# Splitting the out-projection's weights on GpSimd instead of ACT, DVE and SP

## The chip, the cores and the metric

The kernel runs on one core of one Trainium2 chip. Its time is the device time of one execution in microseconds, lower is better; each kernel is run several times and the median is given. The engines are TensorE (PE: matmuls), VectorE (DVE), ScalarE (ACT), GpSimd (POOL) and SyncE (SP). Each engine works its own queue in order. SP's queue does nothing here but issue DMA transfers; POOL's queue holds arithmetic and DMA issues together.

## What is computed

One decoder layer on a sequence of 1024 tokens and a model width of 1024, in float32. The core of the reference, cut down:

```python
h = rms_norm(x, pre_g)
z = einsum('bsd,de->bse', h, w_in)                 # in-projection, width 7184
qa, ka, va, ga, qb, kb, vb, gb, gk_low = split_columns(z)
oa = diff_attention(qa, ka, va, lam)               # 8 heads, two softmax maps each
oa = rms_norm(oa, subln_g) * (1 - lam_init) * silu(ga)
ob = gla_chunked(qb, kb, vb, log_a)                # 4 heads, gated linear attention
ob = rms_norm(ob, gla_g) * silu(gb)
y = einsum('bse,ed->bsd', concatenate([oa, ob]), w_out)   # out-projection, 2048 x 1024
return x + rms_norm(y, post_g)
```

## The kernel before

TensorE multiplies numbers of a shortened float32 form (`fp32r`). To keep the precision, each operand is split into two such parts: the high part is the value cast to `fp32r` (`act.copy(hi, raw)`), the low part is the value minus the high part (`dve.tensor_tensor(lo, raw, hi, subtract)`). A product is then three matmuls: high by high, low by high, high by low.

The in-projection runs from the start to about 630 us. It goes through the columns of `w_in` in pairs of blocks, with a scheme of seven block products for each pair in place of eight (the steps n = 1, 2, 5, 6, 4, 7, 3 of the list `order`). For each step, `make_weights` takes a raw block of `w_in` (tile `w_raw`), for some steps forms a difference of blocks on DVE (line 296), and splits it (line 315 on ACT, line 316 on DVE) into a tile `w`. There are five such tiles (`NRING = 5`), and `go` prepares the weights of up to three steps ahead before it issues a step's matmuls (`multiply`, line 117). A step is 12 matmuls with 512 columns (24 with 256 columns for the values).

Results leave PSUM in `step`: ACT copies one product to an SBUF tile `s` (line 427), and DVE adds another product from PSUM to it (line 440) into a tile `c`. Then `take` finishes the block (for instance scale, gate or split) and SP stores it to DRAM. The tile `c` comes from a group of four buffers with the tag "c":

```python
def t_c(name, dt=F32):
    return t2k("c", 4, name, dt)
```

Beside the in-projection runs the gated linear attention (`gla`, fed by `fill`): among its steps is a causal mask on POOL (`pool.affine_select`, line 775, tile `gan`), which TensorE's products `gpo` read later.

In the same stage the weights of the out-projection, `w_out`, are split ahead of time, so that the later stage can load finished high and low parts. This is `wo_step`. The matrix is cut into 32 pieces of 128 rows and 512 columns (256 KB each). The steps n = 2 and n = 4 of a pair load one piece into the tile `wo_raw`, of which there is one buffer (tag "t4", `bufs=1`); the steps n = 1 and n = 6 split the piece that is loaded: the high part goes to a tile `wo_hi`, taken from the four buffers of tag "c", the low part is written over the raw piece. Both are stored to DRAM (`wod`). So the next load waits until the low part's store is done.

Which buffer a tile gets, and the order of the instructions on each queue, is not written by hand. A planner goes through the program at build time with its own estimates of each instruction's cost, and lets the instruction go first that is ready and comes earlier in the program. Only TensorE's matmuls and a few instructions (`tc.keep_in_program_order`) hold the order of the program. At run time every queue keeps the order that was planned, and each instruction waits by semaphores for what it needs.

The finished parts are read back by `weights` (line 910): the pieces of the rows 1024 to 2047 on POOL's queue from about 602 us, the others on SP's from about 806 us. From 630 us on come the attention (scores, softmax, values) and the out-projection in turns.

Of the kernel before, what the change touches and what calls it, by code (L numbers as in the profile page):

```python
# [11 lines left out]
ALU = mybir.AluOpType  # L12
PSUM = bass.MemoryType.PSUM

P = 128
# [16 lines left out]
def hymba_kernel(  # L32
# [21 lines left out]
    act, dve, pool, pe, sp = nc.scalar, nc.vector, nc.gpsimd, nc.tensor, nc.sync  # L54

    def fp(t):
        return t.bitcast(F32)

    def cols(half):
        return slice(half * 512, half * 512 + 512)  # L60
# [38 lines left out]
    wod = [tc.dram_tile([2, P, D], F32, name=f"wo{e}_d") for e in range(2 * D // P)]  # L99
# [60 lines left out]
    def t_c(name, dt=F32):  # L160
        return t2k("c", 4, name, dt)
# [418 lines left out]
    def wo_step(n):  # L580
        if n in (1, 6) and wo_open:
            e, dh, raw = wo_open.pop()
            hi = t_c("wo_hi", F32R)
            act.copy(hi, raw)
            lo = raw.bitcast(F32R)
            dve.tensor_tensor(lo, raw, fp(hi), ALU.subtract)
            for t, src in enumerate((hi, lo)):
                sp.dma_start(wod[e][t][:, cols(dh)], fp(src))
        if n in (2, 4) and wo_todo:
            e, dh = wo_todo.pop(0)  # L590
            raw = ap.tile([P, 512], F32, tag="t4", name="wo_raw", bufs=1)
            sp.dma_start(raw, w_out[0, e * P : (e + 1) * P, cols(dh)])
            wo_open.append((e, dh, raw))

    def go(n):
        for _ in range(n):
            i = made[0]
            if i == len(order):
                return
            made[0] = i + 1  # L600
            for a in range(4):
                prepare(i + a)
            step(i)
            if order[i][0] > EARLY and not (wide(order[i][0]) and order[i][0] % 2):
                wo_step(order[i][1])
            if fill and next(fill[0], 0) == 0:
                fill.pop(0)
# [918 lines left out]
```

## Time and profile before

| | us |
|---|---|
| median of 3 runs | 980.15 |
| lowest and highest of them | 979.73 and 980.77 |
| the profiled execution's own time | 979.08 |
| its span in the profile | 977.4 |

Engine busy times in the profile are sums over instructions. A line such as "L584 ACT CAST wo_hi<-wo_raw 128x512" names the line of the kernel, the engine, the operation, the tile that is written and the tile that is read, and the shape (partitions x elements). Where a wait is shown with "<-", the name behind the arrow is what ended it. A DMA's busy time on its queue is only the issue; the time to landing is given apart. The granted clock of TensorE is given as a share of the full one.

### The profile page before, as it was taken

To read this page: it belongs to the slowest core of one execution; us is meant where nothing else is said; L and a number is where in the kernel's file an instruction comes from. 1 tells how busy PE (TensorE), PEld (TensorE's weight loads), DVE (VectorE), ACT (ScalarE), POOL (GpSimd) and SP (SyncE) were. 2 spreads that over 40 slices of the span, in tenths; PEclk is the share of its full clock that TensorE was granted. 3 is DMA by queue.
4 is the path that set the end of the run, shared out by engine and by line. 5 is a ranking of instruction groups with operands and counts; after the bars stand their busy time and mean duration, and the time that the engine had idled before them with its cause. 6 is when DMAs were issued, how large, how long until landed. Compare 5 with 4: busy or idle time off the path is not lost.

```text
span 977.4 us, 15766 instructions
## 1 busy us (share of the span) xinstructions
PE 956.7 (98%) x5338; PEld 830.4 (85%) x5338; DVE 735.4 (75%) x1452; ACT 600.5 (61%) x1164; POOL 142.9 (15%) x158
## 2 busy tenths in 40 slices
PE   5999999999999999999999999999999999999997
PEld 5998988888889998999888888878888888888785
DVE  6887597789866667686786876487888888898554
ACT  8742455487357455454665775366776687887773
POOL 4300000000000010000200002121322222443321
PEclk9999999999999999999999999999999999999999
DMA  9432446656774868897987866987656669994677
GB/s 345 151 110 91 139 135 205 231 179 225 238 247 162 264 187 286 254 294 229 293 259 243 273 202 191 407 269 272 197 186 228 240 199 344 340 294 105 151 208 147
DMA packets 152593, 220.45 MB, mean 226 GB/s; under 512 B 17104, under 2 KB 83664, under 8 KB 152416
## 3 DMA queue, kind: packets, MB, share of 16 engines
q1 hardware_dynamic: 146176, 203.71, 64.1%
q0 software_dynamic: 6336, 15.73, 7.0%
q8 instruction: 42, 0.69, 0.3%
q14 instruction: 39, 0.32, 0.1%
HBM read 133.93 MB, written 88.60 MB: 228 GB/s over the span
## 4 chain that ended last, share of the span: by engine, by line
PE 95%; DVE 2%; ACT 1%; DMA 1%; issue 1%; POOL 0%; SPq 0%; DVEq 0%; ACTq 0%; POOLq 0%
PE x L117 24%; PE y L117 15%; PE z L117 15%; PE ypart L117 13%; PE sc L117 7%; PE po L117 5%; PE yps L117 4%; PE wtr L120 3%; PE gpo L117 3%; PE kv L117 1%; PE gkl_ps L117 1%; PE pa L117 1%; DMA x<-in_x_dram 1%; PE xT L120 1%; DVE s_lo L548 0%
## 5 line engine op out<-in xcount | busy, mean ns | idle before, releaser
L315 ACT CAST w<-w_raw 128x512 fp32r<-128x512 f32 (+1 forms) x164 | 112.4, 688 | 94.7 <-PE y L117 44.1
L316 DVE TENSOR_TENSOR w<-w_raw,w 128x512 fp32r<-128x512 f32 (+1 forms) x164 | 126.7, 774 | 50.1 <-ACT w L315 43.3
L1049 ACT ACTIVATE p<-p,stt 128x896 f32<-128x896 f32 (+7 forms) x128 | 99.3, 777 | 36.7 <-DVE stt L1039 33.9
L427 ACT COPY s<-x 128x512 f32<-128x512 f32 x84 | 49.1, 585 | 84.4 <-PE x L117 84.3
L775 POOL TENSOR_SCALAR_AFFINE_SELECT gan<-gan 128x512 f32<-128x512 f32 x8 | 16.5, 2060 | 485.4 <-ACT gan L774 449.8
L296 DVE TENSOR_TENSOR w_raw<-w_raw 128x512 f32<-128x512 f32 (+1 forms) x96 | 75.9, 791 | 13.9 <-DMA w_raw<-in_w_in_dram 12.6
L1039 DVE CUSTOM_DVE_ANT_0 p<-sc,maskt 128x512 f32<-128x512 f32 (+3 forms) x128 | 74.3, 585 | 14.5 <-PE sc L117 13.3
L117 PE MATMUL ypart<-wo_hi,m_hi 128*128 128x512 f32 x192 | 79.5, 414 | 0.1
L117 PE MATMUL y<-h_hi,w 128*128 128x512 f32 x320 | 79.6, 391 | 0.0
L117 PE MATMUL z<-s_hi,w 128*128 128x512 f32 x320 | 79.6, 391 | 0.0
L117 PE MATMUL x<-s_hi,w 128*128 128x512 f32 x320 | 79.6, 391 | 0.0
L1055 POOL TENSOR_SCALAR p<-p,stt,lam 128x1024 f32<-128x1024 f32 (+3 forms) x64 | 56.2, 879 | 146.9 <-DVE stt L1054 141.9
L117 PE MATMUL ypart<-wo_hi,m_lo 128*128 128x512 f32 x192 | 75.5, 393 | 0.0
L117 PE MATMUL ypart<-wo_lo,m_hi 128*128 128x512 f32 x192 | 75.4, 393 | 0.0
L117 PE MATMUL sc<-k,q 128*128 128x512 f32 (+1 forms) x192 | 69.0, 363 | 1.3 <-DVE stt L1039 1.2
L117 PEld LDWEIGHTS x<-s_hi,w 128*128 128x128 f32 x320 | 59.7, 188 | 12.2
L117 PEld LDWEIGHTS y<-h_hi,w 128*128 128x128 f32 x320 | 59.6, 188 | 12.2
L117 PEld LDWEIGHTS z<-s_hi,w 128*128 128x128 f32 x320 | 59.5, 188 | 12.0
L117 PE MATMUL sc<-ks,q 128*128 128x512 f32 (+1 forms) x192 | 66.1, 347 | 0.0
L1097 ACT CAST wt_hi<-wtr 128x512 fp32r<-128x512 f32 (+1 forms) x80 | 42.7, 534 | 24.6 <-PE wtr L120 23.8
L1098 DVE TENSOR_TENSOR wt_lo<-wtr,wt_hi 128x512 fp32r<-128x512 f32 (+1 forms) x80 | 50.7, 633 | 8.6 <-ACT wt_hi L1097 8.0
L1058 DVE SCALAR_TENSOR_TENSOR p<-p,stt,p 128x1024 f32<-128x1024 f32 (+3 forms) x64 | 52.1, 814 | 4.1 <-POOL p L1055 3.9
(226 smaller groups left out, 2247.7 us busy)
## 6 DMA issues: line engine op xcount, KB each, us to landing
w_raw<-in_w_in_dram SPq DMA_DIRECT2D x56, 512.0 KB, 4.7
wo_raw<-in_w_out_dram SPq DMA_DIRECT2D x32, 256.0 KB, 3.0
wo_d<-wo_hi SPq DMA_DIRECT2D x32, 256.0 KB, 2.8
wo_d<-wo_raw SPq DMA_DIRECT2D x32, 256.0 KB, 3.8
q<-q_d SPq DMA_DIRECT2D x32, 256.0 KB, 4.7
k<-k_d SPq DMA_DIRECT2D x32, 256.0 KB, 5.7
ks<-k_d SPq DMA_DIRECT2D x64, 128.0 KB, 6.2
v<-v_d SPq DMA_DIRECT2D x16, 512.0 KB, 7.0
```

Of the source, the lines that this page charges most:

```text
L117: tc.keep_in_program_order(pe.matmul(*a, **k))
L120: tc.keep_in_program_order(pe.transpose(dst, src, ident))
L296: dve.tensor_tensor(dst, a, b, ALU.subtract)
L315: act.copy(w[0], src)
L316: dve.tensor_tensor(w[1], src, fp(w[0]), ALU.subtract)
L427: act.copy(b[k], ps)
L1039: ins = dve.tensor_tensor_reduce(p[:, a:e], sc[:, : e - a], maskt[:, NZ + P - (e - a) :] if last else maskt[:, : e - a], 1.0, 3e38 if i == ...
L1049: act.activation(p[:, :n], p[:, :n], AF.Exp, bias=st[:, m : m + 1], scale=-1.0, accum_out=st[:, 2 + m : 3 + m],)
L1055: pool.tensor_scalar(p1[:, :n], p1[:, :n], st[:, 5:6], lam, ALU.mult, ALU.mult)
L1058: dve.scalar_tensor_tensor(p0[:, :n], p0[:, :n], st[:, 4:5], p1[:, :n], ALU.mult, ALU.subtract)
L1097: act.copy(hi[:, :n], pt[:, :n])
L1098: dve.tensor_tensor(lo[:, :n], pt[:, :n], fp(hi[:, :n]), ALU.subtract)
```

## The change

The 32 pieces of `w_out` are handled by POOL alone. The load of a piece, the cast to the high part, the difference that is the low part and the two stores all go to POOL's queue: 32 loads, 32 casts, 32 differences and 64 stores. ACT, DVE and SP have none of it. The buffers, their tags and their counts, and the places of the calls in the program stay as they are.

```diff
@@ wo_step @@
         if n in (1, 6) and wo_open:
             e, dh, raw = wo_open.pop()
             hi = t_c("wo_hi", F32R)
-            act.copy(hi, raw)
+            pool.tensor_copy(hi, raw)
             lo = raw.bitcast(F32R)
-            dve.tensor_tensor(lo, raw, fp(hi), ALU.subtract)
+            pool.tensor_tensor(lo, raw, fp(hi), ALU.subtract)
             for t, src in enumerate((hi, lo)):
-                sp.dma_start(wod[e][t][:, cols(dh)], fp(src))
+                pool.dma_start(wod[e][t][:, cols(dh)], fp(src))
         if n in (2, 4) and wo_todo:
             e, dh = wo_todo.pop(0)
             raw = ap.tile([P, 512], F32, tag="t4", name="wo_raw", bufs=1)
-            sp.dma_start(raw, w_out[0, e * P : (e + 1) * P, cols(dh)])
+            pool.dma_start(raw, w_out[0, e * P : (e + 1) * P, cols(dh)])
             wo_open.append((e, dh, raw))
```

## The prediction

> **What bounds the kernel now.** I read the page's head first, then the waits of TensorE, then the busy time by stretches. The head gives the span and the engines' shares.
>
> ```profile
> span 977.4 us, 15766 instructions
> PE 956.7 (98%) x5338; PEld 830.4 (85%) x5338; DVE 735.4 (75%) x1452; ACT 600.5 (61%) x1164; POOL 142.9 (15%) x158
> ```
>
> The view of waits, for TensorE alone (engine and line, what it waited for, us in total, times, longest):
>
> ```profile
> PE xT L120 <- DVE x L482: 9.4, 4, 7.2
> PE y L117 <- DVE s L565: 1.3, 1, 1.3
> PE sc L117 <- DVE stt L1039: 1.2, 2, 0.9
> PE y L117 <- ACT s L427: 0.7, 1, 0.7
> PE x L117 <- ACT h_hi L521: 0.6, 1, 0.6
> PE po L117 <- ACT wt_hi L1097: 0.5, 1, 0.5
> ```
>
> The stretches. The splits of the out-projection's weights run from 158 to 556 us.
>
> ```profile
> core 0: us, PE busy (x) PEld busy (x) DVE busy (x) ACT busy (x) POOL busy (x), PEclk, DMA share, GB/s
> 0.00:30.00 30.00, 20.02 (x125) 18.22 (x126) 19.81 (x40) 24.37 (x47) 16.90 (x23) 1.00 0.99 345
> 158.00:300.00 142.00, 142.00 (x656) 118.60 (x655) 110.90 (x178) 83.42 (x145) 0.66 (x1) 1.00 0.66 223
> 300.00:560.00 260.00, 260.00 (x1662) 236.24 (x1661) 188.29 (x286) 146.36 (x256) 15.82 (x7) 1.00 0.79 251
> 632.00:977.00 345.00, 336.84 (x1743) 283.62 (x1741) 267.70 (x719) 245.84 (x553) 98.09 (x106) 1.00 0.76 229
> ```
>
> TensorE is the bound. While the splits run it is busy 142.00 of 142 us and 260.00 of 260 us, at the full clock (1.00). DVE and ACT work beside it with room left (110.90 and 83.42 of 142). POOL is nearly idle there: 0.66 us of work in 142. The reader should take one thing from this: there is no idle time of TensorE between 158 and 560 us for the change to take away, only idle time that it can add.
>
> **What is taken off ACT and DVE.** The tile view of the raw weight gives the two arithmetic steps (ns min/median/max).
>
> ```profile
> L584 ACT CAST wo_hi<-wo_raw x32: 603/621/622, 158.4 to 553.8; 128x512 fp32r<-128x512 f32 x32
> L586 DVE TENSOR_TENSOR wo_raw<-wo_raw,wo_hi x32: 680/687/695, 159.2 to 554.4; 128x512 fp32r<-128x512 f32 x32
> ```
>
> ACT loses 32 x 0.621 = 19.9 us and DVE 32 x 0.687 = 22.0 us. Both lie wholly beside a TensorE that never waits here, so I count them at 0. If that cover were missing, 22 us is the most they could be worth.
>
> **What is taken off SP.** 96 transfers leave SP's queue: 32 loads and 64 stores. From the waits of SP:
>
> ```profile
> SPq L588 <- ACT wo_hi L584: 53.5, 22, 5.8
> SPq L592 <- DMA wo_d<-wo_raw: 52.3, 27, 4.2
> ```
>
> SP stood 105.8 us behind these two steps. Queued behind them were the next in-projection weights and the stores of finished blocks. All of that still came in time, since TensorE shows no wait, so this too counts 0.
>
> **What POOL gets.** On POOL one piece is a serial chain, because the raw buffer is single and everything is on one in-order queue: load lands, cast, difference, two stores issued, the store of the low part lands, next load. I price each link by the nearest rows. Transfers first (KB each, median us from issue to landing):
>
> ```profile
> wo_raw<-in_w_out_dram SPq DMA_DIRECT2D x32, 256.0 KB, 3.0
> wo_d<-wo_hi SPq DMA_DIRECT2D x32, 256.0 KB, 2.8
> wo_d<-wo_raw SPq DMA_DIRECT2D x32, 256.0 KB, 3.8
> ...
> y_d<-yst SPq DMA_DIRECT2D x16, 256.0 KB, 4.4
> ...
> y_d<-yst POOLq DMA_DIRECT2D x16, 256.0 KB, 5.1
> ```
>
> The last two rows are the same 256 KB from the two queues: POOL's lands 5.1 - 4.4 = 0.7 us later (it also accumulates, so 0.7 may be too much). I add 0.7: load 3.7, high part 3.5, low part 4.5. The bounds are 0 and the whole 5.1 for each. The Trainium skill, in "DMA: Bandwidth & Descriptors", section "Latency and other measured facts", gives a first byte at about 1 us from GpSimd's queue and 0.6 us from SP's, so about 0.4 us later; by that the chain below would be 11.5 us and the loss about 2.6 us instead of 11.1.
>
> POOL's arithmetic, by shape (count, busy us, mean ns):
>
> ```profile
> L1147 POOL TENSOR_TENSOR gate<-r,gate 128x512 f32<-128x512 f32 x14 | 18.5, 1323 | 41.0 <-DVE r L1146 31.2 <-DVE stt L1054 9.8
> L775 POOL TENSOR_SCALAR_AFFINE_SELECT gan<-gan 128x512 f32<-128x512 f32 x8 | 16.5, 2060 | 485.4 <-ACT gan L774 449.8 <-DMA wo_d<-wo_hi 35.5
> ...
> L910 POOL DMA_DIRECT2D wo_lo<-wo_d x8 | 4.3, 534 | 3.0 <-PE x L117 1.4 <-PE y L117 0.8 <-DMA wo_lo<-wo_d 0.7
> ```
>
> No POOL cast of 128x512 stands in the trace. The nearest row is L775: one input of the same size, in the same stage. Its spread matters:
>
> ```profile
> L775 POOL TENSOR_SCALAR_AFFINE_SELECT gan<-gan x8: 659/1397/5553, 280.2 to 543.7; 128x512 f32<-128x512 f32 x8
> ```
>
> Alone it takes 0.66 us, in the median 1.40, at worst 5.55. The worst one shows why:
>
> ```profile
> 470.46 5.55 POOL L775 TENSOR_SCALAR_AFFINE_SELECT gan<-gan 128x512 f32<-128x512 f32 x1 [37.79 <-ACT gan L774]
> ```
>
> ```profile
> 474.23 1.29 DVE L316 TENSOR_TENSOR w<-w_raw,w 128x512 fp32r<-128x512 f32 x2
> 475.55 1.73 DVE L296 TENSOR_TENSOR w_raw<-w_raw 128x512 f32<-128x512 f32 x2
> ```
>
> DVE ran differences of two SBUF operands back to back up to 475.5; POOL ended 0.5 us after the first gap, and the next DVE pair took 1.73 us instead of 1.29. So POOL waits for a gap in such DVE work, and then DVE waits for POOL. The Trainium skill says the same in "SBUF — State Buffer", section "Who interferes with whom": a VectorE instruction with two SBUF inputs and a GpSimd instruction that reads SBUF shut each other out for a whole instruction; the trace agrees with its 5.55 us. What it would do to DVE is a rival below.
>
> I take 1.4 us for the cast (0.66 to 2.06) and 1.3 + 0.7 = 2.0 us for the difference (1.3 alone; 0.7 is the same wait, 1.40 - 0.66; at most 1.3 + 1.4). An issue from POOL is 0.53 us. The chain: 3.7 + 1.4 + 2.0 + 0.53 + 4.5 = 12.13 us a piece. The bounds: 3.0 + 0.66 + 1.3 + 0.53 + 3.8 = 9.3 and 5.1 + 2.06 + 2.7 + 0.53 + 5.1 = 15.5.
>
> **Against what pace.** The casts of before, from the timeline (start, us): piece 1, piece 15 and the last, piece 32.
>
> ```profile
> 158.43 0.62 ACT L584 CAST wo_hi<-wo_raw 128x512 fp32r<-128x512 f32 x1
> ```
>
> ```profile
> 300.13 0.60 ACT L584 CAST wo_hi<-wo_raw 128x512 fp32r<-128x512 f32 x1
> ```
>
> ```profile
> 553.79 0.62 ACT L584 CAST wo_hi<-wo_raw 128x512 fp32r<-128x512 f32 x1 [1.67 <-DMA wo_raw<-in_w_out_dram]
> ```
>
> The first 14 intervals take 141.7 us, 10.1 each; the later 17 take 253.7, 14.9 each. A chain of 12.13 falls behind by 2.01 us a piece (12.13 - 10.12) in the first stretch, 28.1 us by its end, and catches up in the second. Pieces late in themselves cost nothing: what they make is read after 600 us. The way to TensorE is the high part's buffer. It is one of four of tag "c", shared with the sums of finished blocks. Its reuse, from the timeline (in between come three other takings of such a buffer):
>
> ```profile
> 196.71 0.62 ACT L584 CAST wo_hi<-wo_raw 128x512 fp32r<-128x512 f32 x1
> ```
>
> ```profile
> 212.81 0.69 DVE L440 TENSOR_TENSOR c<-y,s 128x512 f32<-128x512 f32 x1 [1.57 <-ACT s L427]
> ```
>
> The buffer is wanted again 16.1 us after its cast began; on POOL it is held 1.4 + 2.0 + 3.5 = 6.9 us. So 9.2 us of lag are free. Beyond it the sum L440 waits on DVE, and behind it stand the weights' low parts (L316). Weights are made up to 3 steps ahead; a step is half of this row of the chain of waits:
>
> ```profile
> 185.06 5.44 PE x L117 x24
> ```
>
> That is 3 x 2.72 = 8.2 us more cover. What is left reaches TensorE: 28.1 - 9.2 - 8.2 = 10.7 us.
>
> Also queued behind POOL's waits are the eight masks L775. The worst of before began at 470.46, and its reader is
>
> ```profile
> 482.42 0.38 PE L117 MATMUL gpo<-gan,gv 128*128 128x128 f32 x2
> ```
>
> so a mask may come 12.0 - 0.66 = 11.3 us late; a piece's load or store wait (3.7 or 4.5 us) is inside that.
>
> The first load of all goes out late, since SP has much to issue before it:
>
> ```profile
> 19.82 0.60 SPq L592 DMA_DIRECT2D wo_raw<-in_w_out_dram  x1
> ```
>
> On POOL it has nothing before it and may go out while the first rows of x arrive. 256 KB at 345 GB/s is 0.76 us; TensorE's first wait (9.4 us, for x) could grow by 0 to 0.76. I take 0.4.
>
> **The sum.** 10.7 + 0.4 = 11.1 us. The profiled execution took 979.08 us (span 977.4 and 1.68 around it); the median of the runs is 980.15, so 1.07 us above it. On the median: 980.15 + 11.1 = 991.3 us. With the short chain of 9.3 nothing falls behind and nothing is lost; with 15.5 it is 5.4 x 14 - 17 = 58 us.
>
> **The rivals.**
> First, no change: the order of every queue is worked out by a planner at build time. If it prices POOL's chain about as long as it is, it gives later buffers to the pieces and no one waits; 32 x 12.1 = 387 us fit into the 395 from 158.43 to 553.79. A chain under 10.1 + 17.4 / 14 = 11.3 us gives the same. For it speaks the low bound of 9.3 and that lateness is free; against it that ACT stood before the last cast for the load to land (1.67 us in the row of 553.79), so the order of before already expects transfers quicker than they are. Time: 980.15 + 0.4, about 980.5.
> Second, DVE becomes late by the shared access, not by the buffer. While POOL works on a piece (1.3 + 0.66 us, waits not counted) DVE's two-operand work stands; 0.69 us of DVE goes away. That is 1.3 us more of DVE a piece at worst, 18 in the first 14: 129 of 142 us. It still fits on average; if two thirds of it fall where DVE has no room, 12 - 8.2 = 4 us are lost: 984.
> Third, the masks: if POOL lags by more than 11.3 us, each of eight makes TensorE wait, say 2.5 us: 20 us, 1000.
> Fourth, faster: SP, freed of 105.8 us, and ACT and DVE bring everything earlier. The waits that TensorE still has behind the first piece are sc 1.2 and po 0.5: 1.7 us, and 345 - 336.84 = 8.2 us of idle in the last stretch, of which a third might move by another order: at best 3 us, 977. It decides if POOL's chain stays under 10.1 and the start doesn't pay.
>
> **How the numbers follow.** The forecast, a chain too long that holds the buffers, 0.50; no change 0.33; DVE 0.08; masks 0.04; faster 0.05. A difference of 0.2% (2 us) is about what a measurement of this kernel can tell from no change. Slower by more: 0.50 + 0.08 + 0.04 = 0.62; within: 0.33; faster: 0.05. The forecast's own range is 983 to 1015 (chains of 11.5 to 13.8); with no change in it the range is 979 to 1015, which leaves out the faster case and the longer chains, some 0.1 more.
>
> **What would show it.** Right: a chain of 11.5 us or more from load to load on POOL in 158 to 300; new waits of DVE L440 for the transfer wo_d<-wo_hi; TensorE waits for DVE or ACT of about 10 us in all between 158 and 320; later steps of before shifted by as much. Wrong: TensorE still at 142 of 142 us; or the loss in another stretch (after 632, or at the start by more than 0.8); or TensorE waiting for L775.

## The result: 983.3 us, slower by 0.29%, and the profile after

| | before | after |
|---|---|---|
| median of 6 runs each, us | 979.94 | 983.28 |
| lowest and highest, us | 979.08, 980.77 | 982.41, 984.87 |
| ratio of the times, 95% interval | | 1.0029 [1.0018, 1.0039] |
| profiled execution: own time, span, us | 979.08, 977.4 | 983.59, 981.8 |

The change costs 3.3 us. The forecast had the sign, and 11.1 us. The page's head after, the span and the engines' totals:

```profile
span 981.8 us, 15766 instructions
PE 959.2 (98%) x5338; PEld 830.7 (85%) x5338; DVE 745.8 (76%) x1420; ACT 585.5 (60%) x1132; POOL 268.2 (27%) x318
```

Look at DVE. It was 735.4 us and gave away 32 differences, 22.0 us, so 713.4 were to be expected. It shows 745.8. Its remaining work became 32.4 us longer, 1.01 us for each piece. That is more than the 0.69 it was relieved of.

The view of waits for TensorE after (us in total, times, longest):

```profile
PE xT L120 <- DVE x L482: 8.9, 4, 7.2
PE x L117 <- ACT s L427: 1.6, 1, 1.6
...
PE z L117 <- DVE c L440: 0.3, 1, 0.3
PE z L117 <- DVE c L411: 0.3, 1, 0.3
```

The second, third and fourth of these lines are new: 2.2 us in three waits. They are short. The stretches:

```profile
0.00:30.00 30.00, 20.19 (x118) 18.17 (x119) 19.28 (x39) 24.36 (x47) 18.42 (x24) 1.00 1.00 356
...
158.00:300.00 142.00, 140.10 (x637) 115.81 (x636) 114.14 (x162) 70.10 (x121) 54.05 (x65) 1.00 0.63 207
300.00:560.00 260.00, 259.69 (x1650) 235.09 (x1649) 191.77 (x268) 140.56 (x241) 81.83 (x97) 1.00 0.79 253
```

TensorE, 142.00 of 142 before, has 140.10 now; in the next stretch 259.69 of 260. DVE went up from 110.90 to 114.14 in the first stretch although it has 14 differences less to do.

TensorE executes the same instructions in the same order in every kernel of this study, so two traces can be laid beside each other one matmul at a time. The table gives by how much a kernel's matmuls start later than in the trace of before, at some points of before's time (us). It is worked out from the starts in the traces; each is one execution.

| kernel | 30 | 150 | 220 | 246 | 335 | 420 | 560 | 595 | 660 |
|---|---|---|---|---|---|---|---|---|---|
| after | +0.9 | +0.8 | +0.8 | +3.6 | +4.1 | +4.1 | +4.6 | +4.6 | +4.4 |
| noread11 | +0.7 | +0.7 | +0.7 | +0.7 | +0.7 | +0.9 | +0.9 | +0.9 | +0.6 |
| own_hi | -0.4 | +3.2 | +3.2 | +3.7 | +3.7 | +5.1 | +5.1 | +5.1 | +4.7 |
| own_twice | +0.4 | +5.9 | +6.1 | +8.2 | +8.2 | +9.2 | +9.5 | +9.5 | +10.0 |
| late89 | 0.0 | 0.0 | 0.0 | 0.0 | 0.0 | 0.0 | 0.0 | +7.1 | +7.8 |
| late89_own | -0.4 | +3.0 | +3.0 | +3.9 | +3.9 | +5.5 | +5.5 | +5.5 | +5.1 |
| own_noread | +0.3 | +1.5 | +1.5 | +1.5 | +9.3 | +9.3 | +9.3 | +9.3 | +8.9 |
| dma_again | -0.5 | +0.7 | +0.7 | +0.7 | +0.8 | +2.6 | +2.6 | +2.6 | +2.3 |
| cast_sp | -0.8 | -0.8 | -0.8 | -0.8 | -0.8 | -0.8 | -0.8 | -0.8 | -0.8 |
| diff_sp | -0.9 | -0.9 | -0.9 | +0.3 | +0.3 | +2.2 | +2.2 | +2.2 | +2.5 |

After: 0.9 us are there by 30 us, and 2.8 come between 220 and 246. In that second place POOL, DVE, ACT and TensorE read as follows. POOL's timeline, one whole piece from load to load (start, us):

```profile
236.06 0.54 POOL L592 DMA_DIRECT2D wo_raw<-in_w_out_dram  x1 [5.33 <-DMA wo_d<-wo_raw]
239.13 0.70 POOL L584 CAST wo_hi<-wo_raw 128x512 fp32r<-128x512 f32 x1 [2.52 <-DMA wo_raw<-in_w_out_dram]
239.91 1.60 POOL L586 TENSOR_TENSOR wo_raw<-wo_raw,wo_hi 128x512 fp32r<-128x512 f32 x1
241.47 0.56 POOL L588 DMA_DIRECT2D wo_d<-wo_hi  x1
242.02 0.54 POOL L588 DMA_DIRECT2D wo_d<-wo_raw  x1
245.84 0.54 POOL L592 DMA_DIRECT2D wo_raw<-in_w_out_dram  x1 [3.27 <-DMA wo_d<-wo_raw]
```

DVE in the same microseconds:

```profile
238.67 0.68 DVE L375 TENSOR_TENSOR c<-c,g 128x512 f32<-128x512 f32 x1
239.27 1.10 DVE L382 SCALAR_TENSOR_TENSOR c<-c,b 128x512 f32<-128x512 f32 x1
240.29 1.77 DVE L375 TENSOR_TENSOR c<-c,g 128x512 f32<-128x512 f32 x1
...
243.80 0.68 DVE L440 TENSOR_TENSOR c<-z,s 128x512 f32<-128x512 f32 x1
```

The same operation of line 375 takes 0.68 us at 238.67 and 1.77 us at 240.29, while POOL's difference runs (239.91 to 241.51). With line 382 (1.10; 0.69 at most in before), which began beside POOL's cast, DVE loses 1.09 + 0.41 = 1.5 us in this one piece. It has no gap from 238 to 245.6 in which to make it up. Then ACT, and TensorE behind it:

```profile
244.51 0.63 ACT L372 ACTIVATE g<-c 128x512 f32<-128x512 f32 x1 [4.47 <-DVE c L440]
...
245.71 0.57 ACT L427 COPY s<-x 128x512 f32<-128x512 f32 x1
```

```profile
246.33 2.12 PE L117 MATMUL x<-s_hi,w 128*128 128x512 f32 x8 [1.57 <-ACT s L427]
```

ACT's gate (line 372) waits for DVE's late sum, the copy that TensorE needs stands two places behind it in ACT's queue, and TensorE stops for 1.57 us: about the 1.5 us that DVE was held up. This is one reading of one trace. The experiments ask whether it is the cause.

### The profile page after: what moved, and what is told of

Its sections match the earlier page's. It is cut to its first block, busy times and chain, and to the rows that moved or that the text cites. A ratio compares the mean times of both kernels' runs of the same rounds, so it can differ in the third digit from the quotient of the medians.

```text
span 981.8 us, 15766 instructions
## 1 busy us (share of the span) xinstructions
PE 959.2 (98%) x5338; PEld 830.7 (85%) x5338; DVE 745.8 (76%) x1420; ACT 585.5 (60%) x1132; POOL 268.2 (27%) x318
## 4 chain that ended last, share of the span: by engine, by line
PE 86%; DVE 7%; ACT 3%; issue 2%; DMA 2%; SPq 0%; POOL 0%; DVEq 0%; ACTq 0%; POOLq 0%
PE x L117 21%; PE ypart L117 13%; PE y L117 13%; PE z L117 13%; PE sc L117 7%; PE po L117 5%; PE yps L117 4%; PE wtr L120 3%; PE gpo L117 3%; DVE w L316 1%; PE kv L117 1%; PE gkl_ps L117 1%; DVE w_raw L296 1%; PE pa L117 1%; DMA x<-in_x_dram 1%
## 5 line engine op out<-in xcount | busy, mean ns | idle before, releaser
L316 DVE TENSOR_TENSOR w<-w_raw,w 128x512 fp32r<-128x512 f32 (+1 forms) x164 | 138.7, 848 | 59.5 <-ACT w L315 48.5
L584 POOL CAST wo_hi<-wo_raw 128x512 fp32r<-128x512 f32 x32 | 32.4, 1012 | 240.3 <-DMA q_d<-c 113.1
L296 DVE TENSOR_TENSOR w_raw<-w_raw 128x512 f32<-128x512 f32 (+1 forms) x96 | 80.0, 833 | 20.9 <-DMA w_raw<-in_w_in_dram 19.3
```

The source lines that it names most:

```text
L296: dve.tensor_tensor(dst, a, b, ALU.subtract)
L316: dve.tensor_tensor(w[1], src, fp(w[0]), ALU.subtract)
L584: pool.tensor_copy(hi, raw)
```

## The experiments

Four theories are named in the expectations. Theory 1: POOL's reads of SBUF hold up DVE. Theory 2: the forecast's, POOL's chain of loads and stores holds a shared buffer too long. Theory 3: the planner's other order on ACT and DVE. Theory 4 (for one kernel): loads from POOL's queue land late and hold up ACT's queue. Each group of kernels ran on one chip beside the kernel before; the ratios are to it.

### Only the reads, in the order of before

To the kernel before is added POOL work that nobody uses, behind each low store; all other queues have the order of before. `dummy_read` has two operations: the first reads the constant tile `maskt` and one column of a piece's high half, the second both tiles whole. `dummy_write` has one-column work and four writes of zeros.

```diff
+ pool.tensor_scalar(maskt[:, :512], maskt[:, :512], fp(hi)[:, 0:1], None, ALU.mult)       # dummy_read
+ pool.tensor_tensor(maskt[:, :512], maskt[:, :512], fp(hi), ALU.mult)
+ for _ in range(4): pool.memset(maskt[:, :512], 0.0)                                       # dummy_write
```

> The kernel before, plus 32 pairs of POOL instructions that read the high part and a constant tile of zeros and write the zeros back: one of one tile input, one of two, 128x512 each, as the change's cast and difference. ACT, DVE, SP and PE keep the order of before; the pieces stay on ACT, DVE and SP. Theory 1 (POOL's reads shut DVE out): each pair costs DVE about 1.0 us, as the change did (745.84 - 735.39 + 22.0 = 32.4 us in 32 pieces); DVE, which keeps its own 22 us, is busy about 768 us and the time is 983 to 988. Theory 2 (the pieces' chain on POOL is late and holds a buffer of tag c): no such chain here, 980 within 1. Theory 3 (the planner's other order on ACT and DVE): the order is that of before, 980 within 1.

> As dummy_read, but POOL only writes: after each piece a one-column product and four memsets of 128x512, about as long on POOL. Theory 1: writes alone shut nobody out; DVE busy within 3 us of before's 735.4, time 980 within 1. Theories 2 and 3: 980 within 1 too. If POOL's mere work cost time, it would be as slow as dummy_read.

Measured: dummy_read 981.85 us, ratio 1.0023 [1.0011, 1.0034]; dummy_write 980.28 us, 1.0005 [0.9994, 1.0016]. The two heads' lines, reads first:

```profile
PE 957.5 (98%) x5338; PEld 829.9 (85%) x5338; DVE 762.0 (78%) x1452; ACT 599.9 (61%) x1164; POOL 272.7 (28%) x222
```

```profile
PE 958.0 (98%) x5338; PEld 831.0 (85%) x5338; DVE 735.7 (75%) x1452; ACT 600.1 (61%) x1164; POOL 230.9 (24%) x318
```

Reads make DVE 26.6 us longer (0.83 us a pair of operations), writes do nothing to it. Theory 1's effect exists, without another order or another queue for the DMAs. Its price in the total is 2.0 us there, less than theory 1 expected, and 1.6 us more than dummy_write, with intervals that overlap a little. Where in the kernel it is paid the traces don't settle: dummy_read's largest loss, 2.1 us at 410 us, is at a place where dummy_write's trace, of an execution 1.7 us above its median, loses 1.4 without such reads.

### The start

`first_sp` is the change with the first load alone back on SP's queue.

```diff
- pool.dma_start(raw, w_out[0, e * P : (e + 1) * P, cols(dh)])
+ (sp if (e, dh) == (8, 0) else pool).dma_start(raw, w_out[0, e * P : (e + 1) * P, cols(dh)])
```

> The change with the first of the 32 loads put back on SP's queue. The trace of after shows TensorE 0.7 us behind from 20.6 us on. Early-load theory: that 0.7 goes, the rest stays: 982.5. Rival (the start's shift is from elsewhere): 983.3. The loss from 223 to 246 us of about 2.9 us stays in both.

Measured: 983.7 us, 1.004 [1.0025, 1.0055]. Its trace, of its slowest execution, starts without the shift (-0.4 us at 30 and 220 us instead of +0.9 and +0.8), loses 2.7 us between 220 and 246 as the change does, and loses more later. Of the 0.9 us only a step of 0.5, between 13.5 and 16 us, goes with the early load: all eleven traces with the first load on POOL have it, the six others with it on SP don't. The rest differs from trace to trace: dma_again, own_hi and late89, with the same early load, stand at -0.5, -0.4 and 0.0 us at 30 us. The total shows nothing of it here.

### The change without reads

First try, `memset`: cast and difference are replaced by writes of zeros, so the stored parts are zero.

```diff
- pool.tensor_copy(hi, raw)
+ pool.memset(fp(hi), 0.0)
- pool.tensor_tensor(lo, raw, fp(hi), ALU.subtract)
+ pool.memset(raw, 0.0); pool.memset(raw, 0.0)
```

> The change with POOL's cast and difference replaced by one and two memsets (no reading; the stored weights are zeros): loads, stores, chain and buffers on POOL as in the change. Theory 1: DVE is no longer shut out, busy about 713 us, the loss between 223 and 246 us goes: 980.5 to 981.5. Theories 2 and 3 (late chain and held buffer; another order of the queues): 983 within 1.

Measured: 1006.45 us, 1.0275 [1.025, 1.0301]. Its waits of DVE show why:

```profile
DVE c L440 <- DMA wo_d<-wo_hi: 30.3, 3, 22.9
```

Here a high half no longer depends on its load, and the planner gave it a shared buffer long before POOL's queue could write and store it. DVE stood 22.9 us behind one store. So the experiment says nothing on the reads in the total, but it shows the forecast's mechanism at work and what it can cost. DVE's total, 715.8 us, is not stretched (713.4 expected).

Second, `noread11` keeps every dependence: one column is still cast and subtracted, the other 511 are written with zeros.

```diff
- pool.tensor_copy(hi, raw)
+ pool.tensor_copy(hi[:, :1], raw[:, :1]); pool.memset(fp(hi)[:, 1:], 0.0)
- pool.tensor_tensor(lo, raw, fp(hi), ALU.subtract)
+ pool.tensor_tensor(lo[:, :1], raw[:, :1], fp(hi)[:, :1], ALU.subtract); pool.memset(raw[:, 1:], 0.0)
```

> The change with GpSimd's cast and difference cut to one column each (so that both still wait for the load and for the buffer) and a write of zeros over the other 511 columns; loads, stores, buffers and queue as in the change. The weights that come out are zero but for one column in each piece. Theory 1 (GpSimd's reads of SBUF hold up VectorE): VectorE's busy time falls from 745.8 to about 713 us, the 2.9 us between 223 and 246 us go, total 980 to 981 us. Theory 2 (GpSimd's chain of waits keeps its buffer too long): the chain is as long as in the change, total about 983. Theory 3 (the planner's other order on ACT and DVE at 223 to 246 us): total about 983 if the order there is the change's own.

Measured: 979.97 us, 1.0009 [0.9997, 1.0021]: no loss that can be told from none. The head's line, and the stretch:

```profile
PE 957.8 (98%) x5338; PEld 831.0 (85%) x5338; DVE 717.6 (73%) x1420; ACT 586.4 (60%) x1132; POOL 245.3 (25%) x382
```

```profile
158.00:300.00 142.00, 142.00 (x656) 118.60 (x655) 103.98 (x165) 76.12 (x130) 43.20 (x95) 1.00 0.67 222
```

Loads, stores, buffers and the queue are the change's own, and DVE waited for a high store seven times, 26.0 us in all, without TensorE noticing; TensorE is back at 142.00 of 142. The early start stays (+0.7 us). What went with the reads is the loss at 220 to 246 us. One reserve: from about 220 us on the planner's order on ACT and DVE is not quite that of the change (the products of line 375 that are at 238.67 and 240.29 in the change stand earlier in DVE's queue), so this alone doesn't exclude theory 3. No run has the change's order at this place without the reads; kernels with noread11's order and the reads are compared with it below.

### The buffer

`own_hi` gives the high halves a buffer of their own, in the zero part of the constant tile `maskt`, which nobody needs in this stage.

```diff
- hi = t_c("wo_hi", F32R)
+ hi = maskt[:, :512].bitcast(F32R)
...
  assert not wo_todo and not wo_open
+ pool.memset(maskt[:, :512], 0.0)
```

> The change with the high halves in a buffer of their own, which nobody else takes. Theory 2 (the shared buffer is held by GpSimd's queue): DVE line 440 no longer waits for the high store, total about 980. Theory 1 (reads hold up VectorE): VectorE busy about 746 us as in the change, total stays at 982.5 to 984.

Measured: 984.38 us, 1.0045 [1.0033, 1.0057]. With no shared buffer at all the total stays as high, which speaks against theory 2. But the loss sits in another place: the pieces now run from 9.5 us on, +3.6 us come between 30 and 150 us in the table and only 0.5 between 220 and 246. Some of it is not DVE's either:

```profile
PE xT L120 <- POOL xt L482: 1.6, 1, 1.6
```

At 30.7 us TensorE waits for POOL's own line 482, while no piece is worked on. That the buffer costs the change little is read more directly from the change itself, where DVE waited for a high store once, at 520 us.

`own_noread` is own_hi without reads (the stored parts are zero), `shared_noread` the same with the shared buffer. On TensorE, DVE, ACT and SP both have own_hi's instructions in own_hi's order.

```diff
- pool.tensor_copy(hi, raw)
+ g = pool.memset(raw, 0.0)
- pool.tensor_tensor(lo, raw, fp(hi), ALU.subtract)
+ with tc.issue_after(g.ins): pool.memset(fp(hi), 0.0)
```

> own_hi with GpSimd's cast and difference turned into two writes of zeros (first over the piece, which waits for the load, then over the high halves); TensorE, VectorE, ACT and SP have the same instructions in the same order as own_hi, and the loads and stores stay on GpSimd's queue. The weights that come out are zero. Theory 1 (GpSimd's reads hold up VectorE): the 4.4 us that own_hi loses go, total 980 to 981 us, VectorE busy about 714 instead of 742 us. Theory 3 (the order on ACT and VectorE, or the DMAs on GpSimd's queue): total 983 to 984 as own_hi.

Measured: 989.26 us, 1.0113 [1.0076, 1.015], a miss for both theories. TensorE's waits and POOL's timeline:

```profile
PE gpo L117 <- POOL gan L775: 4.8, 1, 4.8
```

```profile
300.33 0.53 POOL L940 MEMSET maskt<- 128x512 f32 x1 [4.25 <-DMA wo_d<-maskt]
300.81 0.64 POOL L775 TENSOR_SCALAR_AFFINE_SELECT gan<-gan 128x512 f32<-128x512 f32 x1
```

The last zeroing of the constant tile waits for the last store, and the causal mask of line 775, which TensorE needs, stands behind it: the forecast's third rival, made by the experiment's own line 940. Up to there the kernel had lost 1.5 us, own_hi 3.7, of which 1.7 at POOL's line 482; so this pair says little on the reads in the total. It does on DVE: with the order kept its busy time falls from 742.0 to 716.4 us.

> The change with GpSimd's cast and difference turned into two writes of zeros, the first over the piece (waits for the load), the second over the high halves in the shared buffer; TensorE, VectorE, ACT and SP have the same instructions in the same order as own_hi. The weights that come out are zero. Theory 1 (reads hold up VectorE): 980 to 981 us, VectorE busy about 714 us. Theory 3 (order, or DMAs on GpSimd's queue): 983 to 984.4 us as own_hi.

Measured: 1004.69 us, 1.0253 [1.0229, 1.0277], a miss again, and the same fate as memset:

```profile
DVE c L440 <- DMA wo_d<-wo_hi: 18.7, 1, 18.7
```

### Twice the reads

`own_twice` is own_hi with a second difference and a second cast in each piece, whose results are written over.

```diff
+ pool.tensor_tensor(hi, raw, fp(raw), ALU.subtract); pool.tensor_copy(hi, raw)
  pool.tensor_copy(hi, raw)
```

> own_hi with a second difference and a second cast in each piece on GpSimd, whose results are written over; nearly the same order elsewhere. Theory 1 (reads): VectorE busy rises by about 25 to 30 us over own_hi's 742 us, and the total by 3 to 6 us over own_hi's 984.4. Theory 3 (order, DMAs): total as own_hi, unless GpSimd's chain falls behind.

Measured: 989.66 us, 1.0111 [1.0098, 1.0124]; own_hi stood at 1.0045. The heads' lines of own_hi and own_twice:

```profile
PE 957.4 (97%) x5338; PEld 829.6 (84%) x5338; DVE 742.0 (76%) x1420; ACT 586.1 (60%) x1132; POOL 271.9 (28%) x319
```

```profile
PE 960.2 (97%) x5338; PEld 830.9 (84%) x5338; DVE 758.8 (77%) x1420; ACT 586.0 (59%) x1132; POOL 339.8 (34%) x383
```

Doubling the reads takes the loss from 0.45% to 1.11%, as theory 1 said. DVE grew by 16.8 us, less than the 25 to 30 expected. The two kernels have no shared buffer and nearly the same order (two instructions each of DVE and of ACT stand elsewhere), so here the reads cost time with theories 2 and 3 all but held still. What is new in the trace are stops behind DVE, or behind ACT's copy: 2.2 us at 59 us (0.5 in own_hi), 1.0 at 224 and 0.8 at 232.

### Which half: the DMAs or the arithmetic

`arith` is the change with load and stores on SP; `dma` the change with the cast on ACT and the difference on DVE.

```diff
- pool.dma_start(...)                                   # arith: both places
+ sp.dma_start(...)
- pool.tensor_copy(hi, raw)                             # dma
+ act.copy(hi, raw)
- pool.tensor_tensor(lo, raw, fp(hi), ALU.subtract)
+ dve.tensor_tensor(lo, raw, fp(hi), ALU.subtract)
```

> The change with cast and difference on GpSimd, but load and stores on SP's queue as before. Theory 1 (reads by GpSimd): VectorE busy about 746 us, total about 983. Theory 2 (queue and landings of GpSimd's DMAs): total about 980.

> The change with the cast on ACT and the difference on DVE as before, but load and stores on GpSimd's queue. Theory 1 (reads by GpSimd): VectorE busy about 735 us as before, total 980 to 981. Theory 2 (queue and landings): the buffer is held as long as in the change, total 983 or more.

Measured: arith 981.46 us, 1.0015 [1.0004, 1.0025]; dma 982.44 us, 1.0033 [1.002, 1.0046]. The second was not what theory 1 expected: DVE is not stretched there (735.0 us), and it loses as much as the whole change. Its trace was of its fastest execution, so it was run again.

> The run called dma once more, for a trace of an execution near its median (the first trace was of its fastest). Theory 4 (the load lands later from GpSimd's queue and holds up the cast on ACT, and what stands behind it there): 982 to 983 us, with waits of ACT line 584 on the load, or of line 427 behind it, where TensorE stops. Theory 1 has nothing to say on it: VectorE busy about 735.

Measured: 982.7 us, 1.0039 [1.0027, 1.0052]. The largest losses in its trace are 1.2 us each: at 30.7 us, where TensorE waits for POOL's line 482 as in own_hi, and at 379 us. POOL and ACT at the second:

```profile
374.56 0.54 POOL L592 DMA_DIRECT2D wo_raw<-in_w_out_dram  x1 [6.28 <-DMA wo_d<-wo_raw]
```

```profile
378.47 0.62 ACT L584 CAST wo_hi<-wo_raw 128x512 fp32r<-128x512 f32 x1 [4.59 <-DMA v_d<-v_hi]
...
380.73 0.57 ACT L427 COPY s<-x 128x512 f32<-128x512 f32 x1
```

The load goes out when the store before it has landed, 6.28 us of POOL's waiting; ACT stands 4.59 us at the cast, and the copy that TensorE needs is behind it. The profile names another transfer as what ended ACT's wait, but that one landed at 378.64, after the cast had begun; the load landed at 378.44. So theory 4 fits this one stop, though no run took that wait away. That the traces show 2.3 of the 3.7 us leaves the rest open. The two halves don't add up to the change (1.9 and 2.8 to 3.7 us, against 3.3), as they need not: with the arithmetic on POOL nobody but POOL stands behind a late load, and noread11, with all its DMAs on POOL, loses nothing that can be told.

### Fewer pieces in the dense place

`late89` begins no piece in the steps of pairs 8 and 9. In its trace POOL works on no piece from 184 to 221 us, and on two between 221 and 246 us.

```diff
- if order[i][0] > EARLY and not (wide(order[i][0]) and order[i][0] % 2):
+ if order[i][0] > EARLY and order[i][0] not in (8, 9) and not (wide(order[i][0]) and order[i][0] % 2):
```

> The change with no piece begun in pairs 8 and 9 (about 196 to 246 us), where VectorE has no gaps; the pieces that stood there come later. Theory 1 (reads cost where VectorE has no slack): the 2.9 us between 223 and 246 us go, total about 980.5 to 981.5. Theory 3 (order): may go either way, since ACT's and VectorE's order changes too; a loss of 3 us that stays speaks for neither alone.

Measured: 989.84 us, 1.0108 [1.0091, 1.0126]. The loss at 220 to 246 us did go (0.0 at 246 and at 560 us), though two pieces are still worked on there, and the order there is noread11's and not the change's: less work for POOL before this place goes with it, but the run alone doesn't say why. And the last pieces now come after 560 us, and there 7 us are lost. DVE, and the stretches (the third number from the end is TensorE's granted clock):

```profile
588.63 0.69 DVE L440 TENSOR_TENSOR c<-z,s 128x512 f32<-128x512 f32 x1 [7.55 <-issue]
```

```profile
580.00:586.00 6.00, 6.00 (x28) 4.95 (x28) 1.08 (x2) 1.61 (x3) 3.13 (x4) 1.00 1.12 349
...
592.00:594.00 2.00, 2.00 (x5) 1.61 (x6) 1.96 (x4) 0.82 (x2) 0.40 (x1) 0.50 0.83 247
...
600.00:610.00 10.00, 10.00 (x46) 8.29 (x45) 8.72 (x14) 6.87 (x13) 4.17 (x6) 1.00 0.45 146
```

POOL issued a high store at 582.87, into DMA engines that are full (share 1.12). It landed at 588.55, and DVE's line 440, whose wait the page can only call "issue", began at 588.63. TensorE stood 4.6 us behind it, and then worked at a clock of 0.50 for some microseconds: the next 12 matmuls started 0.2 us later each, another 2.4 us.

`late89_own` is late89 with own_hi's buffer.

> late89 with the high halves in a buffer of their own. Theory 2 for late89 (VectorE line 440 waits until the high store has landed, and TensorE's 4.6 us standstill brings its clock down to half for some us): no standstill at 586 us, clock 1.00 in 560 to 636, total 982 to 985 us, what the reads cost. If the 8 us have another cause, total 988 to 990.

Measured: 984.29 us, 1.0045 [1.0025, 1.0064]: no standstill after 560 us, and own_hi's loss. So in late89 it was the shared buffer: the forecast's mechanism, at a place where the DMA engines are full.

The traces can now be compared at the change's own place of loss. DVE's instructions between 196 and 246 us are matched with their medians in before, and TensorE's loss is taken between 220 and 246 us:

| kernel | order on ACT and DVE there | DVE longer, us | TensorE's loss, us |
|---|---|---|---|
| noread11, own_noread | noread11's | 0.3, 0.4 | 0.0, 0.0 |
| late89 | noread11's | 2.7 | 0.0 |
| own_hi, late89_own | noread11's | 4.6, 5.4 | 0.5, 0.9 |
| own_twice, arith | noread11's | 6.2, 6.3 | 2.1, 1.4 |
| after, first_sp | the change's | 5.6, 5.6 | 2.8, 2.7 |

With one and the same order TensorE loses nothing without the reads, and more where DVE is held up more: at this place the reads cost time whatever theory 3 adds. The change's order then seems to add to it, by how much no run says.

### Which of the two operations

Matched by line, tiles and shape with before, DVE's instructions between 150 and 570 us in the trace of the change are 31.1 us longer than their medians in before (noread11's 2.6). 24.7 us of this lie in instructions beside POOL's difference alone, nothing in the 39 beside the cast alone, and 5.9 in 22 that began beside the cast and ended beside the difference, as line 382 above. So each was moved alone, all else as before: `cast_sp` has the cast on POOL, `diff_sp` the difference.

```diff
- act.copy(hi, raw)
+ pool.tensor_copy(hi, raw)                              # cast_sp
- dve.tensor_tensor(lo, raw, fp(hi), ALU.subtract)
+ pool.tensor_tensor(lo, raw, fp(hi), ALU.subtract)      # diff_sp
```

> The kernel before with only the cast moved to GpSimd. If only GpSimd's two-input difference holds up VectorE (theory 1, sharpened): VectorE busy 735 to 737 us as before, total 979.5 to 980.5 us, no difference from before. If any read of GpSimd does: VectorE busy about 745 us, total 981 or more.

> The kernel before with only the difference moved to GpSimd. Theory 1, sharpened: VectorE busy 740 to 746 us (713 without the 22 us that leave, and 25 to 32 stretched), total 981 to 983 us as arith. If the two reads share the blame: VectorE about 730, total 980 to 981.

Measured: cast_sp 979.97 us, 1.0004 [0.9996, 1.0013]; diff_sp 984.46 us, 1.0049 [1.0036, 1.0063]. The heads' lines and the first stretch, cast_sp first:

```profile
PE 956.9 (98%) x5338; PEld 830.2 (85%) x5338; DVE 741.7 (76%) x1452; ACT 586.2 (60%) x1132; POOL 165.3 (17%) x190
158.00:300.00 142.00, 142.00 (x656) 118.62 (x655) 112.55 (x179) 75.94 (x130) 13.28 (x15) 1.00 0.67 222
```

```profile
PE 957.1 (98%) x5338; PEld 830.1 (85%) x5338; DVE 739.6 (75%) x1420; ACT 600.3 (61%) x1164; POOL 182.2 (19%) x190
158.00:300.00 142.00, 141.04 (x651) 117.51 (x650) 113.21 (x163) 82.23 (x144) 20.49 (x15) 1.00 0.66 220
```

The cast on POOL costs nothing that the total shows. The difference on POOL costs 0.49% with no other step moved: no DMA is on POOL's queue, and DVE waits for no store of a piece. DVE with 32 differences less is at 739.6 us, 26.2 above 713.4; matched as above, 21.7 of it lie beside the difference, 0.7 us a piece. The cast stretches DVE a little (741.7 against 735.4; 735 to 737 was expected): 2.5 us lie beside it, nearly all in seven instructions that are 0.3 to 0.4 us longer each, and most of the rest lies where no piece is worked on. These two runs say which step of the change costs: the two-input subtraction on POOL. How much of the 4.9 us is DVE's hold-up they leave open. The trace of diff_sp, of its fastest execution, loses 1.1 us at 224 us behind ACT's copy, as the change does, and 1.6 us at 410 us, where dummy_write's trace loses nearly as much without such reads:

```profile
PE gpo L117 <- DVE gu L803: 1.4, 1, 1.4
```

The two runs also speak against theory 3 as the whole cause: the queues of ACT and DVE are reordered in cast_sp at least as much as in diff_sp, and cast_sp loses nothing.

## Why the prediction was wrong, point by point

**TensorE is the bound, and relief of ACT, DVE and SP is worth nothing.** Right. noread11 has all the relief and no gain: 1.0009 [0.9997, 1.0021].

**POOL's chain, 12.13 us a piece: the step that failed.** The transfers' medians were priced well (3.7, 3.5 and 4.5 us; KB each and median landing after):

```profile
wo_raw<-in_w_out_dram POOLq DMA_DIRECT2D x32, 256.0 KB, 3.8
wo_d<-wo_hi POOLq DMA_DIRECT2D x32, 256.0 KB, 3.2
wo_d<-wo_raw POOLq DMA_DIRECT2D x32, 256.0 KB, 4.5
```

The arithmetic was too dear: 1.4 and 2.0 us against medians of 0.72 and 1.61.

```profile
L584 POOL CAST wo_hi<-wo_raw x32: 605/716/4637, 157.2 to 564.6; 128x512 fp32r<-128x512 f32 x32
L586 POOL TENSOR_TENSOR wo_raw<-wo_raw,wo_hi x32: 1264/1608/2075, 157.9 to 565.6; 128x512 fp32r<-128x512 f32 x32
```

Both prices came from the median of an operation, the mask, that had met DVE's work eight times, as if every piece met it in the median. The casts of pieces 1 and 15:

```profile
157.18 0.67 POOL L584 CAST wo_hi<-wo_raw 128x512 fp32r<-128x512 f32 x1 [113.08 <-DMA q_d<-c]
...
312.71 1.15 POOL L584 CAST wo_hi<-wo_raw 128x512 fp32r<-128x512 f32 x1 [2.45 <-DVE sq_hl L835]
```

That is (312.71 - 157.18) / 14 = 11.1 us a piece, between the pace of 10.12 and the forecast's 12.13. The chain did fall behind, but by 155.5 - 141.7 = 13.8 us over the 14 pieces and not by 28.1. The forecast's own cover was 9.2 + 8.2 = 17.4 us; 13.8 lies inside it, so the 10.7 us that should have been left over never were. DVE waited for a high store once,

```profile
DVE c L440 <- DMA wo_d<-wo_hi: 6.1, 1, 6.1
```

at 520 us, and at most 0.5 us of it came through to TensorE. A chain under 11.3 us that costs nothing was the first rival, and 11.1 is inside the stated bounds (9.3 to 15.5); of the two numbers beside each other, 12.13 and a threshold of 11.3, the text trusted the first too much. That the time rose, as forecast, is luck: what raised it is not this chain.

**The mechanism itself** (a shared buffer held until a store lands) was not wrong: memset, shared_noread and late89 pay 7 to 27 us for it, and late89_own takes it away. The change merely stays clear of it.

**The start, 0.4 us (0 to 0.76).** About right: the step that goes with the early load is 0.5 us in the traces. As first_sp shows, the total does not follow it.

**The second rival: right in kind and size, with a chance of 0.08.** DVE held up by POOL's access, 984 us: measured 983.28. Its working had 18 us more of DVE in the first 14 pieces; the stretch shows 114.14 - (110.90 - 14 x 0.69) = 12.9 us for the 13 pieces that fall into it now, 1.0 a piece instead of 1.3. That its 984 comes so close is partly luck, for it spread the loss over the stretch, and the trace has most of it at one stop. It was given that chance because DVE "still fits on average", 129 of 142 us. The stretches of before, taken finer, show the place where it does not:

```profile
200.00:250.00 50.00, 50.00 (x223) 41.39 (x222) 44.73 (x73) 36.57 (x65) 0.00 (x0) 1.00 0.56 192
```

DVE already had 44.73 of 50 us to do, and there, by the reading above, a delay of 1.5 us in one piece passed through ACT's queue to TensorE. The Trainium skill, "SBUF — State Buffer", section "Who interferes with whom", has the rule: a VectorE instruction with two SBUF inputs and a GpSimd instruction that reads SBUF exclude each other. The traces agree for the difference, with up to 1.1 us more on a 0.68 us instruction, and for dummy_write's writes, which cost DVE nothing. The cast, which reads as well, shows it too, with 0.3 to 0.4 us in each of the seven instructions of cast_sp.

**The masks** did not come late in the change; own_noread shows what it costs when one does.

**What stays open.** How much of the change's 3.3 us the planner's order adds: POOL's arithmetic costs 1.9 to 4.9 us over before in the orders tried (arith, dummy_read, diff_sp), and one execution's trace shows 4.4 us for the change. And why DMAs on POOL's queue alone cost 2.8 to 3.7 us when ACT and DVE do the arithmetic; dma_again's trace loses nothing between 220 and 246 us, so this is another loss than the change's.

## What to carry to other kernels

Before moving elementwise work to an idle GpSimd, count what it does to VectorE: a two-input operation of 128x512 there cost VectorE 0.7 to 1.0 us, no less than the 0.69 us that VectorE needs to do it itself, while the one-input cast went over at no cost that the total showed. "Fits on average" is no argument where the busy engine has a stretch without gaps; look at the timeline of that stretch, and at who stands behind its late instruction in the next queue. A chain priced within 10% of the length at which it begins to cost (12.13 against 11.3) has no sign yet: give the two sides like chances.

## What the runs showed that was not expected

A stop of TensorE costs more than its length once it is long enough. After 4.6 us (late89) and 4.8 us (own_noread) without work the granted clock was 0.50, and 2.5 and 3.0 us more were lost (7.1 and 7.8 in the table); the stop of 1.57 us in the change left it at 1.00. The Trainium skill, "TensorE: Matmul & The Clock Gate", section "Part 1: The HAM clock gate (the 'warmup' mystery)", states such a gate, half the clock after an idle window of about 3.4 us; the three stops agree.

POOL's cast pays for meeting DVE too: 0.61 us at best and 4.64 at worst, as the mask's 5.55 us of before.
